# Both halves of an adaLN vector summed by one group of products, two steps after its sums

## The chip, the cores and the metric

The kernel runs on one core of a Trainium2 chip. The core has five engines with a queue of instructions each: TensorE (PE, matmuls), VectorE (DVE), ScalarE (ACT), GpSimd (POOL) and SyncE (SP), which here issues the loads. The metric is the device time of one execution in microseconds.

## What is computed

Two layers of a decoder trunk on `x` of 256 rows by 1024. Each layer runs a first SwiGLU FFN, a token mixer and a second FFN. In front of each of them stands an RMS norm, scaled and shifted by vectors that depend on the condition `c`, and behind each a gate. All of these come from one product per layer:

```python
mod = c_act @ w_ada[l] + b_ada[l]                 # 1024 x 9216
sh1, sc1, g1, sh2, sc2, g2, sh3, sc3, g3 = jnp.split(mod, N_MOD, axis=-1)
x = x + 0.5 * g1 * swiglu(modulate(x, sh1, sc1), ffn1_gate[l], ffn1_up[l], ffn1_down[l])
x = x + g2 * token_mix(modulate(x, sh2, sc2), ...)
x = x + 0.5 * g3 * swiglu(modulate(x, sh3, sc3), ffn2_gate[l], ffn2_up[l], ffn2_down[l])
```

`modulate` is `rms_norm(x) * (1 + scale) + shift`, `swiglu` is `(silu(u @ gate) * (u @ up)) @ down` with 2816 hidden columns. This text calls the nine parts of `mod` chunks 0 to 8. All of it is fp32.

## The kernel before

**Matrix products.** Every fp32 operand is split in two fp32r parts, a rounded high part and the rest. Weights come in loads of up to 1 MB into one of four `raw` buffers (SP, lines 216, 432, 625, 626), and are split there: ACT copies the high part (`whi`, line 177), DVE subtracts it (`wlo`, line 179), each 128x1024 a piece, two pieces a load. PE does three products for each pair of tiles (line 105). A `raw` buffer is free for another load when the last reader on DVE is done, and SP issues loads in one fixed order. A split pair goes into one of seven buffers.

**The vectors of adaLN.** `ada_half` (line 206 on) makes one half, 512 columns, of a chunk: two loads of 1 MB of `w_ada` (line 216), and for each load four scaled additions on DVE into an accumulator `acc` (lines 220 and 222). That leaves 128 partial sums in 128 partitions. Gates (chunks 2, 5 and 8, rows) are then split by ACT (line 229) and DVE (line 230), and two matmuls with a matrix of ones add them up for all partitions; ACT copies the result (line 236). Scales and shifts (columns) go through a `finish`: `column_sums` adds them up with four products of 32 columns into a `tr` bank, eight matmuls in the trace; `pick_columns` takes the wanted elements with a mask on DVE (`mcol`, line 194) and a reduction (`cs`, line 197); `add_bias` writes four columns of `col` (line 203). A `finish` is put in a list and called at the next step of the generator. Ten vectors of columns are made so, in 20 halves.

**Stages.** Chunks 2 to 6 of a layer are made in its first FFN, chunk 7 of layer 0 in its token mixer, and chunk 8 of a layer with chunks 1, 0 and 7 of the next one in its second FFN. (Layer 0's chunks 1 and 0 are made at the start in another way, in `begin`.) Within an FFN the gate and up products run in groups of 256 columns, with one or two steps of the generator (one load of `w_ada` each) per group. Then the down projection runs in two halves of 512 columns (`c = 0, 1`), each of 22 k-tiles in six loads, the last of half size, each load with one step of the generator. Here the six loads of the first half are called D0 to D5, and D6 is the first of the second half. A load feeds 24 matmuls of 128x512. In layer 1's first FFN the chunks come as 2, 3, 4, 5, 6: chunk 4's last half is summed as the gate and up products end, chunks 5 and 6 in the first half of the down projection. At the end of a half the residual is added on DVE (lines 452 and 453).

**What sets the order.** A scheduler orders each engine's queue by its own estimates and by which buffers are free. Each engine does its queue strictly in that order, so an operation that waits holds all that stand behind it on its engine. `acc` has two buffers in the pool `keep`. `sgx` is a tag of the FFN's own pool, with two buffers of the same size, in use by `finish_rows` at the start of an FFN only.

Of the kernel before, what the change touches and what calls it, by code (L numbers as in the profile page):

```python
# [10 lines left out]
F32 = mybir.dt.float32  # L11
# [66 lines left out]
def hybrid_trunk(ctx, tc, t, out):  # L78
# [48 lines left out]
    nc.scalar.activation(cact, c_in, AF.Silu)  # L127
    apart = keep.tile([P, 48], F32, name="apart")
# [57 lines left out]
    def column_sums(ps, vec, a, start, stop):  # L186

        av = a.rearrange("p (j i r) -> p j i r", j=4, i=4)
        for i in range(4):
            mm(ps[32 * i:32 * i + 32, :P].rearrange("p (j r) -> p j r", j=4), vec, av[:, :, i, :], start, stop)  # L190

    def pick_columns(ps):
        m = small.tile([P, 4, 32], F32, name="mcol", tag="mcol", bufs=1)
        nc.vector.tensor_tensor(m, ps[:, :P].rearrange("p (j r) -> p j r", j=4),
                                colmask[:, None, :].to_broadcast([P, 4, 32]), ALU.mult)
        cs = small.tile([P, 4], F32, name="cs", tag="cs", bufs=2)
        nc.vector.tensor_reduce(cs, m, AX.X, ALU.add)
        return cs

    def add_bias(l, ch, n, cs):  # L200
        if (l, ch) not in mods:
            mods[l, ch] = small.tile([P, KD], F32, name="col", tag="col", bufs=8)
        nc.vector.scalar_tensor_tensor(mods[l, ch][:, n * 4:n * 4 + 4], cs, 1.0 if ch in (1, 4, 7) else 0.0,
                                       bcols[:, l, ch * 8 + n * 4:ch * 8 + n * 4 + 4], ALU.add, ALU.add)

    def ada_half(l, ch, n):
        acc = keep.tile([P, 512], F32, name="acc", tag="acc", bufs=2)
        row = ch in (2, 5, 8)
        n0 = ch * D + n * 512
# [15 lines left out]
        if row:  # L225
            if n == 0:
                mods[l, ch] = keep.tile([P, D], F32, name="g", tag="g", bufs=2)
            hi, lo = (scr.tile([P, 512], F32R, name="acc%d" % i, tag="uf", bufs=2) for i in range(2))
# [8 lines left out]
        else:  # L237
            def finish():
                ps = trps()
                column_sums(ps, ones[:, :32].bitcast(F32), acc, True, True)  # L240
                cs = pick_columns(ps)
                add_bias(l, ch, n, cs)
        ada_late.append(finish)
# [4 lines left out]
    def ada_load(chunks):  # L248
        def g():
            for l, ch, n in chunks:  # L250
                for _ in ada_half(l, ch, n):
                    yield
                    while ada_late:
                        ada_late.pop(0)()
# [955 lines left out]
```

## Time and profile before

| what | us |
|---|---|
| median of the three runs | 1186.91 |
| all runs | 2935.22, 1186.91, 1182.08 |
| the profiled execution | 1183.2 |
| its span | 1181.4 |
| granted TensorE clock, mean | 0.999 |

The profile is of one execution. An engine's busy time is given as a share of the span. A wait list names for each engine what it waited for and where. A timeline gives each instruction, or a run of like ones, with its start and duration, and in brackets the idle time ahead of it and what ended it. Consecutive operations on DVE overlap a little, so the distance of two starts says what one of them takes from the engine.

### The profile page before, as it was taken

Reading aid. Unit: us, or ns where it says so; the run is one execution under the profiler, and the core shown is the slowest. Engines: PE = TensorE matmul, PEld = TensorE weight load, DVE = VectorE, ACT = ScalarE, POOL = GpSimd, SP = SyncE. Lnnn points to the kernel's source line nnn. Section 1 sums busy time; section 2 is a strip of 40 time slices with the busy share of each in tenths; the row PEclk is TensorE's granted clock in tenths of the full one; section 3 lists DMA queues with packets and bytes.
Section 4 is the critical chain, followed back from the end, with each engine's and each line's share of the span. In section 5 each row is a group of like instructions: output and inputs, shape, how many; then the busy total and the mean of one; then the engine's idle time right before and its main releaser. Section 6 shows DMA issues by size and latency. Waiting matters only on the chain.

```text
span 1181.4 us, 20214 instructions
## 1 busy us (share of the span) xinstructions
PE 1145.7 (97%) x7886; PEld 1005.9 (85%) x7886; DVE 939.1 (79%) x1889; ACT 642.6 (54%) x1156; POOL 2.5 (0%) x16
## 2 busy tenths in 40 slices
PE   4999999999999999999999999999999999999997
PEld 3799987789967889997879999777997778999985
DVE  4999998778888898798578879975878888865553
ACT  4544544647676564444455534366677756554441
POOL 0000000000000000000000000000000000000000
PEclk9999999999999999999999999999999999999999
DMA  9989999695623578988839979975664354886530
GB/s 330 337 286 330 345 343 332 206 262 174 178 86 102 195 230 290 311 285 314 291 107 295 311 238 360 338 243 167 182 183 108 105 165 157 288 267 211 183 138 36
DMA packets 201970, 274.95 MB, mean 233 GB/s; under 512 B 13613, under 2 KB 119815, under 8 KB 201875
## 3 DMA queue, kind: packets, MB, share of 16 engines
q1 hardware_dynamic: 201119, 273.02, 70.9%
q8 instruction: 62, 1.02, 0.4%
q10 hardware_dynamic: 756, 0.64, 0.2%
q14 instruction: 33, 0.27, 0.1%
HBM read 272.60 MB, written 1.05 MB: 232 GB/s over the span
## 4 chain that ended last, share of the span: by engine, by line
PE 72%; DVE 13%; DMA 8%; ACT 3%; issue 3%; SPq 1%; DVEq 0%; ACTq 0%
PE mm L105 64%; DVE wlo L179 5%; DMA raw<-in_w_ada 4%; DMA raw<-in_ffn_up 3%; PE tr L108 3%; DVE acc L222 3%; PE sc L105 2%; PE po L105 2%; ACT whi L177 1%; PE tr L105 1%; DMA raw<-in_ffn_down 1%; DVE win L724 1%; DVE kd L746 0%; ACT junk L293 0%; DVE hf L494 0%
## 5 line engine op out<-in xcount | busy, mean ns | idle before, releaser
L179 DVE TENSOR_TENSOR wlo<-raw,whi 128x1024 fp32r<-128x1024 f32 (+5 forms) x400 | 423.0, 1073 | 118.0 <-ACT whi L177 115.2
L177 ACT ACTIVATE whi<-raw 128x1024 fp32r<-128x1024 f32 (+5 forms) x400 | 364.3, 936 | 232.4 <-PE mm L105 98.5
L105 PE MATMUL mm<-uhi,whi 128*128 128x256 f32 x1248 | 346.2, 277 | 0.0
L105 PE MATMUL mm<-uhi,wlo 128*128 128x256 f32 x1248 | 345.0, 276 | 0.7 <-DVE wlo L179 0.7
L105 PE MATMUL mm<-ulo,whi 128*128 128x256 f32 x1248 | 344.9, 276 | 0.0
L105 PEld LDWEIGHTS mm<-uhi,whi 128*128 128x128 f32 x1248 | 234.2, 188 | 2.4 <-issue 1.2
L105 PEld LDWEIGHTS mm<-uhi,wlo 128*128 128x128 f32 x1248 | 234.2, 188 | 1.1 <-DVE wlo L179 1.1
L105 PEld LDWEIGHTS mm<-ulo,whi 128*128 128x128 f32 x1248 | 234.4, 188 | 0.5
L222 DVE SCALAR_TENSOR_TENSOR acc<-raw,cact,acc 128x512 f32<-128x512 f32 x224 | 166.9, 747 | 8.7 <-DMA raw<-in_w_ada 5.7
L105 PE MATMUL mm<-whi,hh 128*128 128x512 f32 x352 | 138.2, 393 | 0.0
L105 PE MATMUL mm<-wlo,hh 128*128 128x512 f32 x352 | 137.3, 390 | 0.2 <-DVE wlo L179 0.2
L105 PE MATMUL mm<-whi,hl 128*128 128x512 f32 x352 | 137.1, 389 | 0.0
L105 PE MATMUL mm<-whi,uhi 128*128 128x512 f32 (+3 forms) x336 | 126.3, 378 | 4.4 <-ACT uhi L554 2.6
L105 PE MATMUL mm<-whi,ulo 128*128 128x512 f32 (+3 forms) x336 | 126.3, 377 | 1.5 <-DVE ulo L342 1.5
L105 PE MATMUL mm<-wlo,uhi 128*128 128x512 f32 (+3 forms) x336 | 125.1, 373 | 0.0
L495 ACT ACTIVATE hh<-hf 128x256 fp32r<-128x256 f32 x70 | 29.2, 417 | 103.4 <-DVE hf L494 103.3
L105 PEld LDWEIGHTS mm<-whi,hh 128*128 128x128 f32 x352 | 66.1, 188 | 15.1 <-issue 1.6
L105 PEld LDWEIGHTS mm<-wlo,hh 128*128 128x128 f32 x352 | 66.1, 188 | 14.2 <-DVE wlo L179 0.8
L105 PEld LDWEIGHTS mm<-whi,hl 128*128 128x128 f32 x352 | 66.1, 188 | 13.7
L105 PEld LDWEIGHTS mm<-whi,uhi 128*128 128x128 f32 x336 | 63.3, 189 | 16.1 <-ACT uhi L554 3.0
L105 PEld LDWEIGHTS mm<-whi,ulo 128*128 128x128 f32 x336 | 63.6, 189 | 12.1 <-DVE ulo L342 3.3
L105 PEld LDWEIGHTS mm<-wlo,uhi 128*128 128x128 f32 x336 | 63.6, 189 | 9.5 <-DVE wlo L179 0.2
(248 smaller groups left out, 1327.5 us busy)
## 6 DMA issues: line engine op xcount, KB each, us to landing
raw<-in_w_ada SPq DMA_DIRECT2D x72, 1024.0 KB, 9.0
raw<-in_ffn_gate SPq DMA_DIRECT2D x41, 1024.0 KB, 7.1
raw<-in_ffn_up SPq DMA_DIRECT2D x41, 1024.0 KB, 6.5
raw<-in_ffn_down SPq DMA_DIRECT2D x40, 1024.0 KB, 8.1
raw<-in_w_in SPq DMA_DIRECT2D x18, 1024.0 KB, 6.6
raw<-in_w_in SPq DMA_DIRECT2D x16, 512.0 KB, 6.4
raw<-in_w_out SPq DMA_DIRECT2D x8, 1024.0 KB, 5.1
raw<-in_ffn_down SPq DMA_DIRECT2D x8, 512.0 KB
```

What stands on the lines that cost most here:

```text
L105: last_mm[0] = nc.tensor.matmul(o, a, b, start=start, stop=stop)
L108: nc.tensor.transpose(o, a, ident)
L177: nc.scalar.activation(a, s, AF.Copy)
L179: nc.vector.tensor_tensor(b, s, a.bitcast(F32), ALU.subtract)
L222: nc.vector.scalar_tensor_tensor(acc, rv[:, jj, :], cj, binit if j + jj == 0 else acc, ALU.mult, ALU.add)
L495: nc.scalar.activation(h[0][:, f, :], hf32, AF.Copy)
L724: nc.vector.tensor_tensor(win[i][jj * 64:(jj + 1) * 64, 8 * a:8 * a + 8, g, :], pv[g * 64:(g + 1) * 64, jj, :, a:a + 15], cols[0][jj * 64: ...
```

## The change

`finish` is made once per vector, when both halves are summed. It has eight products in one group, one masked product of 128x256, one reduction to eight columns and one addition of the bias. It is called two steps of the generator behind the end of the sums; the rows' stays at one. Both accumulators are held until then. Every second vector takes its accumulators from `sgx` while an FFN is open, the others from `acc` in `keep`. The tiles with the tag `uf` (`uf`, the rows' split halves, `win`, `pT`, `fnorm`) move from the pool `scr` to the front of `keep`, which shifts the addresses behind it; five more lines like those shown say `keep` for `scr`. Two pads go.

```diff
@@ -125,6 +125,7 @@
     nc.gpsimd.memset(binit, 0.0)
     cact = const.tile([P, KD], F32, name="cact")
     nc.scalar.activation(cact, c_in, AF.Silu)
+    nc.gpsimd.memset(keep.tile([P, 512], F32, name="uf", tag="uf", bufs=2)[:, :1], 0.0)
     apart = keep.tile([P, 48], F32, name="apart")
     nc.gpsimd.memset(apart, 0.0)
     x = keep.tile([P, NH, D], F32, name="x")
@@ -183,29 +184,35 @@
 
     mods = {}
 
-    def column_sums(ps, vec, a, start, stop):
-
-        av = a.rearrange("p (j i r) -> p j i r", j=4, i=4)
-        for i in range(4):
-            mm(ps[32 * i:32 * i + 32, :P].rearrange("p (j r) -> p j r", j=4), vec, av[:, :, i, :], start, stop)
-
-    def pick_columns(ps):
-        m = small.tile([P, 4, 32], F32, name="mcol", tag="mcol", bufs=1)
-        nc.vector.tensor_tensor(m, ps[:, :P].rearrange("p (j r) -> p j r", j=4),
-                                colmask[:, None, :].to_broadcast([P, 4, 32]), ALU.mult)
-        cs = small.tile([P, 4], F32, name="cs", tag="cs", bufs=2)
-        nc.vector.tensor_reduce(cs, m, AX.X, ALU.add)
+    def column_sums(ps, vec, halves):
+
+        for n, a in enumerate(halves):
+            av = a.rearrange("p (j i r) -> p j i r", j=4, i=4)
+            for i in range(4):
+                mm(ps[32 * i:32 * i + 32, n * P:(n + 1) * P].rearrange("p (j r) -> p j r", j=4), vec, av[:, :, i, :],
+                   True, True)
+
+    def pick_columns(ps, n):
+        m = small.tile([P, KD, 32], F32, name="mcol", tag="mcol", bufs=1)
+        nc.vector.tensor_tensor(m[:, :n], ps[:, :n * 32].rearrange("p (j r) -> p j r", j=n),
+                                colmask[:, None, :].to_broadcast([P, n, 32]), ALU.mult)
+        cs = small.tile([P, KD], F32, name="cs", tag="cs", bufs=2)
+        nc.vector.tensor_reduce(cs[:, :n], m[:, :n], AX.X, ALU.add)
         return cs
 
-    def add_bias(l, ch, n, cs):
-        if (l, ch) not in mods:
-            mods[l, ch] = small.tile([P, KD], F32, name="col", tag="col", bufs=8)
-        nc.vector.scalar_tensor_tensor(mods[l, ch][:, n * 4:n * 4 + 4], cs, 1.0 if ch in (1, 4, 7) else 0.0,
-                                       bcols[:, l, ch * 8 + n * 4:ch * 8 + n * 4 + 4], ALU.add, ALU.add)
+
+    acc_rooms = [None]
+    pairs = [0]
+    held = []
 
     def ada_half(l, ch, n):
-        acc = keep.tile([P, 512], F32, name="acc", tag="acc", bufs=2)
         row = ch in (2, 5, 8)
+        if not row and n == 0:
+            pairs[0] += 1
+        if not row and pairs[0] % 2 == 0 and acc_rooms[0] is not None:
+            acc = acc_rooms[0]()
+        else:
+            acc = keep.tile([P, 512], F32, name="acc", tag="acc", bufs=2)
         n0 = ch * D + n * 512
         wv = t["w_ada"][l].rearrange("(p j) n -> p j n", p=P)
         if row:
@@ -225,7 +232,7 @@
         if row:
             if n == 0:
                 mods[l, ch] = keep.tile([P, D], F32, name="g", tag="g", bufs=2)
-            hi, lo = (scr.tile([P, 512], F32R, name="acc%d" % i, tag="uf", bufs=2) for i in range(2))
+            hi, lo = (keep.tile([P, 512], F32R, name="acc%d" % i, tag="uf", bufs=2) for i in range(2))
             nc.scalar.activation(hi, acc, AF.Copy)
             nc.vector.tensor_tensor(lo, acc, hi.bitcast(F32), ALU.subtract)
 
@@ -235,12 +242,20 @@
                 mm(ps, ones, lo, False, True)
                 nc.scalar.activation(mods[l, ch][:, n * 512:(n + 1) * 512], ps, AF.Copy, scale=1.0 if ch == 5 else 0.5)
         else:
+            held.append(acc)
+            if n == 0:
+                return
+            halves = list(held)
+            held.clear()
+
             def finish():
                 ps = trps()
-                column_sums(ps, ones[:, :32].bitcast(F32), acc, True, True)
-                cs = pick_columns(ps)
-                add_bias(l, ch, n, cs)
-        ada_late.append(finish)
+                column_sums(ps, ones[:, :32].bitcast(F32), halves)
+                cs = pick_columns(ps, KD)
+                mods[l, ch] = small.tile([P, KD], F32, name="col", tag="col", bufs=8)
+                nc.vector.scalar_tensor_tensor(mods[l, ch], cs, 1.0 if ch in (1, 4, 7) else 0.0,
+                                               bcols[:, l, ch * 8:ch * 8 + 8], ALU.add, ALU.add)
+        ada_late.append([1 if row else 2, finish])
 
     ada_late = []
     ada_gen = [None]
@@ -250,10 +265,13 @@
             for l, ch, n in chunks:
                 for _ in ada_half(l, ch, n):
                     yield
-                    while ada_late:
-                        ada_late.pop(0)()
+                    for e in list(ada_late):
+                        e[0] -= 1
+                        if e[0] == 0:
+                            ada_late.remove(e)
+                            e[1]()
             while ada_late:
-                ada_late.pop(0)()
+                ada_late.pop(0)[1]()
         ada_gen[0] = g()
 
     def ada_step(n=1):
@@ -468,6 +486,7 @@
             unit_kinds[:] = ["w"] * 4 + ["f"] * EXTRA
             unit_count[0] = 0
             unit_alloc["f"] = lambda: pool_unit(fu)
+            acc_rooms[0] = lambda: fp.tile([P, 512], F32, name="acc", tag="sgx", bufs=2)
             bank_pools[:] = [psum, fps]
             ada_load(ada_plan)
 
@@ -542,11 +561,11 @@
                     accs[q] = acc
 
                 def operands(q):
-                    cs = pick_columns(sums[q])
+                    cs = pick_columns(sums[q], 4)
                     for i, ch in enumerate((1, 0)):
                         nc.vector.scalar_tensor_tensor(mods[l, ch][:, q * 2:q * 2 + 2], cs[:, i * 2:i * 2 + 2], float(ch),
                                                        bcols[:, l, ch * 8 + q * 2:ch * 8 + q * 2 + 2], ALU.add, ALU.add)
-                    uf = scr.tile([P, 2, S], F32, name="uf", tag="uf", bufs=2)
+                    uf = keep.tile([P, 2, S], F32, name="uf", tag="uf", bufs=2)
                     for i in range(2):
                         k = 2 * q + i
                         nc.vector.tensor_scalar(uf[:, i, :], tps[q][:, i * S:(i + 1) * S], mods[l, 1][:, k:k + 1],
@@ -644,6 +663,7 @@
                 xs_gemm(units, ktiles(h[0]), ktiles(h[1]), 512, evac, 6 if c else 0, last if c else None)
             unit_kinds[:] = ["w"]
             bank_pools[:] = [psum]
+            acc_rooms[0] = None
 
 
     def token_mix(l, uhi, ulo, ada_plan, post):
...
@@ -1147,9 +1167,6 @@
-    pad(scr, "before_uf", 320)
-    pad(small, "behind_uf", 192)
```
What this moves on the engines is shown for three places.

**1. A group of column sums, PE, layer 1's first FFN.** `tr` is the bank of the sums, `acc_7968` chunk 4's second half before, `acc_7630` and `acc_7918` its two halves in the change; `whi_8276` is D0's first split before, `whi_8267` D1's in the change. Before:

```order
L105 MATMUL mm_8193<-uhi_6666,wlo_8223 128x256
L105 MATMUL tr_8260<-acc_7968,ones_83 32x128 [waits PE_49]
L105 MATMUL tr_8260<-acc_7968,ones_83 32x128 x3
L105 MATMUL mm_8256<-whi_8276,hh_6763 128x512 [waits Activation_49]
L105 MATMUL mm_8256<-wlo_8277,hh_6763 128x512 [waits DVE_49]
```

In the change:

```order
L105 MATMUL mm_8196<-whi_8221,hl_6720 128x512
L105 MATMUL tr_8239<-acc_7630,ones_83 32x128 x4
L105 MATMUL tr_8239<-acc_7918,ones_83 32x128 x4
L105 MATMUL mm_8195<-whi_8267,hh_6719 128x512 [waits Activation_49]
L105 MATMUL mm_8195<-wlo_8268,hh_6719 128x512 [waits DVE_49]
```

The group has both halves, and stands behind D0's matmuls instead of ahead of them.

**2. The last half of the vectors, DVE, layer 0's second FFN.** `raw_6344` is the third load of the down projection before, `acc_6305` the last half's accumulator:

```order
L179 TENSOR_TENSOR wlo_6329<-raw_6303,whi_6328 128x1024 [waits PE_49,Activation_49]
...
L179 TENSOR_TENSOR wlo_6364<-raw_6344,whi_6363 128x1024 [waits DMAHW7_49,Activation_49]
L179 TENSOR_TENSOR wlo_6380<-raw_6344,whi_6379 128x1024 [waits PE_49,Activation_49]
...
L220 TENSOR_SCALAR acc_6305<-raw_6306,cact_91 128x512 [waits DMAHW6_49]
...
L222 SCALAR_TENSOR_TENSOR acc_6305<-raw_6306,cact_91,acc_6305 128x512 [waits DVE_49] x2
L222 SCALAR_TENSOR_TENSOR acc_6305<-raw_6357,cact_91,acc_6305 128x512 [waits DMAHW0_49,DVE_49]
L179 TENSOR_TENSOR wlo_6408<-raw_6395,whi_6407 128x1024 [waits DMAHW1_49,Activation_49]
L222 SCALAR_TENSOR_TENSOR acc_6305<-raw_6357,cact_91,acc_6305 128x512 [waits DVE_49]
```

In the change the load is `raw_6346`, the accumulator `acc_6267`:

```order
L180 TENSOR_TENSOR wlo_6291<-raw_6250,whi_6290 128x1024 [waits PE_49,Activation_49]
L227 TENSOR_SCALAR acc_6267<-raw_6268,cact_91 128x512 [waits DMAHW6_49]
...
L229 SCALAR_TENSOR_TENSOR acc_6267<-raw_6308,cact_91,acc_6267 128x512 [waits DMAHW0_49,DVE_49]
...
L229 SCALAR_TENSOR_TENSOR acc_6267<-raw_6308,cact_91,acc_6267 128x512 [waits DVE_49]
L180 TENSOR_TENSOR wlo_6364<-raw_6346,whi_6363 128x1024 [waits DMAHW1_49,Activation_49]
L180 TENSOR_TENSOR wlo_6380<-raw_6346,whi_6379 128x1024 [waits Activation_49]
```

The sums, which stood behind the third load's splits, stand ahead of them; PE's products of them, which stood behind the third load's matmuls, stand ahead of these too.

**3. Chunk 5's sums, layer 1's first FFN.** On DVE before, `raw_8258`, `raw_8308` and `raw_8355` are D0, D1 and D2, `acc_8122` and `acc_8315` chunk 5's halves:

```order
L222 SCALAR_TENSOR_TENSOR acc_8122<-raw_8124,cact_91,binit_89 128x512 [waits DMAHW6_49]
...
L222 SCALAR_TENSOR_TENSOR acc_8122<-raw_8124,cact_91,acc_8122 128x512 [waits DVE_49] x2
...
L179 TENSOR_TENSOR wlo_8277<-raw_8258,whi_8276 128x1024 [waits DMAHW7_49,Activation_49]
L179 TENSOR_TENSOR wlo_8293<-raw_8258,whi_8292 128x1024 [waits PE_49,Activation_49]
L222 SCALAR_TENSOR_TENSOR acc_8122<-raw_8270,cact_91,acc_8122 128x512 [waits DMAHW0_49,DVE_49]
...
L179 TENSOR_TENSOR wlo_8324<-raw_8308,whi_8323 128x1024 [waits DMAHW2_49,Activation_49]
L230 TENSOR_TENSOR acc1_8312<-acc_8122,acc0_8311 128x512 [waits Activation_49]
L179 TENSOR_TENSOR wlo_8340<-raw_8308,whi_8339 128x1024 [waits PE_49,Activation_49]
...
L222 SCALAR_TENSOR_TENSOR acc_8315<-raw_8317,cact_91,binit_89 128x512 [waits DMAHW3_49,DMAHW1_49,DVE_49]
...
L179 TENSOR_TENSOR wlo_8368<-raw_8355,whi_8367 128x1024 [waits DMAHW4_49,Activation_49]
L179 TENSOR_TENSOR wlo_8384<-raw_8355,whi_8383 128x1024 [waits PE_49,Activation_49]
```

In the change `raw_8237`, `raw_8299` and `raw_8343` are D1, D2 and D3, `acc_8061` and `acc_8259` chunk 5's halves:

```order
L180 TENSOR_TENSOR wlo_8268<-raw_8237,whi_8267 128x1024 [waits DMAHW1_49,PE_49,Activation_49]
...
L180 TENSOR_TENSOR wlo_8284<-raw_8237,whi_8283 128x1024 [waits PE_49,Activation_49]
...
L180 TENSOR_TENSOR wlo_8312<-raw_8299,whi_8311 128x1024 [waits DMAHW3_49,Activation_49]
L180 TENSOR_TENSOR wlo_8328<-raw_8299,whi_8327 128x1024 [waits PE_49,Activation_49]
...
L229 SCALAR_TENSOR_TENSOR acc_8061<-raw_8063,cact_91,binit_89 128x512 [waits DMAHW6_49,PE_49]
L197 TENSOR_TENSOR mcol_8248<-tr_8239,tab_87 128x256 [waits PE_49]
...
L229 SCALAR_TENSOR_TENSOR acc_8061<-raw_8063,cact_91,acc_8061 128x512 [waits DVE_49]
...
L229 SCALAR_TENSOR_TENSOR acc_8061<-raw_8199,cact_91,acc_8061 128x512 [waits DMAHW0_49,DVE_49]
...
L237 TENSOR_TENSOR acc1_8256<-acc_8061,acc0_8255 128x512 [waits Activation_49]
...
L180 TENSOR_TENSOR wlo_8357<-raw_8343,whi_8356 128x1024 [waits DMAHW6_49]
```

Chunk 5's first sum has a wait for PE now, for the merged group of place 1, and stands behind D2's two splits, where it stood ahead of D0's. SP's queue, before, from the first load of chunk 5 to D3's predecessor:

```order
L216 DMA raw_8124<-in_w_ada 128x4x512 [waits DMAHW2_49,DVE_49]
L432 DMA raw_8258<-in_ffn1_down 128x4x512 [waits DMAHW3_49,DVE_49]
L216 DMA raw_8270<-in_w_ada 128x4x512 [waits DMAHW4_49,DVE_49,Activation_49]
L432 DMA raw_8308<-in_ffn1_down 128x4x512 [waits DMAHW5_49,DVE_49]
L216 DMA raw_8317<-in_w_ada 128x4x512 [waits DMAHW6_49,DVE_49]
L432 DMA raw_8355<-in_ffn1_down 128x4x512 [waits DMAHW7_49,DVE_49]
L216 DMA raw_8361<-in_w_ada 128x4x512 [waits DMAHW0_49,DVE_49]
L432 DMA raw_8399<-in_ffn1_down 128x4x512 [waits DMAHW2_49,DVE_49]
```

In the change (`raw_8197` is D0):

```order
L223 DMA raw_8063<-in_w_ada 128x4x512 [waits DMAHW1_49,DVE_49]
L450 DMA raw_8197<-in_ffn1_down 128x4x512 [waits DMAHW3_49,DVE_49]
L223 DMA raw_8199<-in_w_ada 128x4x512 [waits DMAHW4_49,DVE_49,Activation_49]
L450 DMA raw_8237<-in_ffn1_down 128x4x512 [waits DMAHW5_49,DVE_49]
L223 DMA raw_8261<-in_w_ada 128x4x512 [waits DMAHW7_49,DVE_49]
L450 DMA raw_8299<-in_ffn1_down 128x4x512 [waits DMAHW1_49,DVE_49]
L223 DMA raw_8305<-in_w_ada 128x4x512 [waits DMAHW3_49,DVE_49]
L450 DMA raw_8343<-in_ffn1_down 128x4x512 [waits DMAHW6_49,DVE_49]
```

The sequence is the same, but a load waits for the landing queue (`DMAHW`) of what its buffer held: D2 waits for queue 1, on which D1 landed (DVE's first row above), and D3 for queue 6, on which chunk 5's first load landed. ACT there, in the change:

```order
L178 ACTIVATE whi_8327<-raw_8299 128x1024 [waits PE_49]
L511 ACTIVATE sg_8189<-mm_8132 128x256 [waits PE_49,Activation_49]
L514 ACTIVATE hh_6719<-hf32_8191 128x256 [waits DVE_49]
L219 DMA binit_89<-in_b_ada 1x512 [waits DVE_49]
...
L178 ACTIVATE whi_8356<-raw_8343 128x1024 [waits DMAHW6_49]
L236 ACTIVATE acc0_8255<-acc_8061 128x512 [waits DVE_49]
L178 ACTIVATE whi_8372<-raw_8343 128x1024 [waits PE_49]
```

ACT's half of the row's sum, `acc0_8255`, stands behind D3's first high part, `whi_8356`.

## Rows read from the trace of the kernel before

**Rows 1.** Page, part 1: busy time, share of the span, instructions

```profile
PE 1145.7 (97%) x7886; PEld 1005.9 (85%) x7886; DVE 939.1 (79%) x1889; ACT 642.6 (54%) x1156; POOL 2.5 (0%) x16
```

**Rows 2.** What PE waited for: us in total, times, longest

```profile
PE tr L105 <- DMA raw<-in_w_ada: 10.1, 2, 9.6
PE tr L105 <- DVE acc L541: 2.9, 1, 2.9
...
PE tr L105 <- DVE acc L222: 1.9, 1, 1.9
```

**Rows 3.** PE's timeline at a column group: start, us, engine, line, operation, count

```profile
731.72 0.28 PE L105 MATMUL mm<-ulo,whi 128*128 128x256 f32 x1
731.83 0.28 PE L105 MATMUL mm<-uhi,wlo 128*128 128x256 f32 x1
732.04 0.43 PE L105 MATMUL tr<-acc,ones 128*32 128x128 f32 x8
732.39 0.50 PE L105 MATMUL mm<-whi,hh 128*128 128x512 f32 x1
```

**Rows 4.** Stretch and its us, busy PE, PEld, DVE, ACT, POOL, clock, DMA share, GB/s

```profile
716.00:744.00 28.00, 27.27 (x190) 24.57 (x189) 27.72 (x43) 14.01 (x21) 0.00 (x0) 1.00 1.03 369
```

**Rows 5.** DVE's timeline, layer 0's second FFN, then layer 1's first

```profile
546.19 2.36 DVE L179 TENSOR_TENSOR wlo<-raw,whi 128x1024 fp32r<-128x1024 f32 x2 [1.71 <-ACT whi L177]
...
735.78 1.22 DVE L179 TENSOR_TENSOR wlo<-raw,whi 128x1024 fp32r<-128x1024 f32 x1
736.92 0.42 DVE L494 TENSOR_TENSOR hf<-mm,sg 128x256 f32<-128x256 f32 x1
...
743.28 0.74 DVE L222 SCALAR_TENSOR_TENSOR acc<-raw,cact,acc 128x512 f32<-128x512 f32 x1
743.94 0.42 DVE L496 TENSOR_TENSOR hl<-hf,hh 128x256 fp32r<-128x256 f32 x1
...
763.25 2.36 DVE L179 TENSOR_TENSOR wlo<-raw,whi 128x1024 fp32r<-128x1024 f32 x2 [0.99 <-ACT whi L177]
...
769.72 0.68 DVE L452 TENSOR_TENSOR rtmp<-mm,g 128x512 f32<-128x512 f32 x1
```

**Rows 6.** PE's timeline, first matmuls of D2, then the second of D6

```profile
743.86 0.39 PE L105 MATMUL mm<-whi,hh 128*128 128x512 f32 x1
744.09 0.39 PE L105 MATMUL mm<-wlo,hh 128*128 128x512 f32 x1
...
764.53 0.50 PE L105 MATMUL mm<-wlo,hh 128*128 128x512 f32 x1 [0.24 <-DVE wlo L179]
```

**Rows 7.** By tile, `cs` and `mcol`: duration in ns, min/median/max

```profile
L197 DVE TENSOR_REDUCE cs<-mcol x24: 272/278/286, 16.4 to 778.1; 128x4 f32<-128x128 f32 x24
L203 DVE SCALAR_TENSOR_TENSOR col<-cs,bcols x20: 148/154/164, 116.0 to 779.4; 128x4 f32<-128x4 f32 x20
...
L194 DVE TENSOR_TENSOR mcol<-tr,tab x24: 277/283/286, 16.1 to 776.1; 128x128 f32<-128x128 f32 x24
```

**Rows 8.** ACT's timeline, layer 1's first FFN

```profile
732.64 1.06 ACT L177 ACTIVATE whi<-raw 128x1024 fp32r<-128x1024 f32 x1 [0.51 <-DMA raw<-in_ffn_down]
734.16 0.63 ACT L229 ACTIVATE acc<-acc 128x512 fp32r<-128x512 f32 x1 [0.46 <-DVE acc L222]
```

**Rows 9.** SP's timeline, D2's and D3's loads issued

```profile
730.71 0.37 SPq L432 DMA_DIRECT2D raw<-in_ffn_down  x1
...
737.03 0.37 SPq L432 DMA_DIRECT2D raw<-in_ffn_down  x1
```

**Rows 10.** Page, part 6: loads, count, KB each, median us from issue to landing

```profile
raw<-in_ffn_down SPq DMA_DIRECT2D x40, 1024.0 KB, 8.1
...
raw<-in_w_out SPq DMA_DIRECT2D x8, 1024.0 KB, 5.1
```

**Rows 11.** Columns as in rows 4, the start and the end of the span

```profile
16.00:18.00 2.00, 0.00 (x0) 0.00 (x0) 1.82 (x7) 0.63 (x2) 0.00 (x0) 1.00 1.09 351
...
1179.00:1181.40 2.40, 0.00 (x0) 0.00 (x0) 0.00 (x0) 0.00 (x0) 0.00 (x0) 0.50 0.45 174
```

More of the change, by code (lines that the diff above doesn't have):

```diff
@@ L326, in rest @@
             for b in bs:
-                uf = scr.tile([P, 4, P], F32, name="uf", tag="uf", bufs=2)
+                uf = keep.tile([P, 4, P], F32, name="uf", tag="uf", bufs=2)
                 ps = trps()
@@ L708, in token_mix @@
                 nc.vector.tensor_scalar_mul(cks[:, hf, :256], cks[:, hf, :256], lr[:, 2 + hf:3 + hf])
-            win = [scr.tile([P, 16, 2, 15], F32, name="win%d" % i, tag="uf", bufs=2) for i in range(2)]
+            win = [keep.tile([P, 16, 2, 15], F32, name="win%d" % i, tag="uf", bufs=2) for i in range(2)]
             r = raw_tile()
@@ L966, in transposed @@
                     tr(pt[:, c * P:(c + 1) * P], b)
-                pT = scr.tile([P, 512], F32, name="pT", tag="uf", bufs=2)
+                pT = keep.tile([P, 512], F32, name="pT", tag="uf", bufs=2)
                 if eng is nc.scalar:
@@ L1130, in final_norm @@
             for c in range(2):
-                fnorm[c] = scr.tile([P, 512], F32, name="fnorm%d" % c, tag="uf", bufs=2)
+                fnorm[c] = keep.tile([P, 512], F32, name="fnorm%d" % c, tag="uf", bufs=2)
                 nc.scalar.dma_start(fnorm[c], t["final_norm"].rearrange("(o n) -> o n", o=1)
```

## The prediction, made before the changed kernel ran

> **What bounds the kernel now.** The page comes first: PE is busy 97% of the span, DVE 79% [rows 1]. So the time is PE's own work plus the few waits of PE, and a change is worth what it takes from or adds to these two. Next PE's list of waits: 10.1 us are the first loads of the start, 2.9 us another wait there, and 1.9 us is one wait of a column sum for its accumulator (`acc L222`) [rows 2], and that wait belongs to the operations the change touches. What one group of column products costs PE is read in PE's timeline: the first product starts 0.21 us after the last matmul ahead of it, the next matmul 0.35 us after that, 0.56 us from one to the other, where the matmuls ahead start 0.11 apart [rows 3]. So one group puts in 0.45 us.
>
> Then the stage where the order moves most, layer 1's first FFN from its last gate and up units into the down projection. From 716 to 744 us DVE is busy 27.7 of 28 us and the DMA engines are full (share 1.03, 369 GB/s) [rows 4]. The reader should see that here three things run without slack: loads, DVE's splits and sums, and PE. PE's lead over DVE is short: D1's second split is through at 736.92, where the next operation starts [rows 5], D2's matmuls begin at 743.86 [rows 6], and at D6 the lead is gone, since PE's second matmul there waits 0.24 us for `wlo` [rows 6], whose split starts at 763.25 after a wait for ACT [rows 5].
>
> The profiled execution took 1183.2 us, of which 1181.4 are the span, so 1.8 us lie around it. The median of the runs shown is 1186.9 (1182.1 the lowest): the sum below starts 3.7 us under it, and I keep it there.
>
> **The change, part by part.**
>
> *Products on PE.* Ten vectors have two groups each, 20 x 0.45 = 9.0 us. A merged group keeps one entry and one exit, and adds four fp32 products. Eight matmuls of a group fill 0.43 us against 0.28 for one alone [rows 3], so seven steps take 0.15 us, eight more some 0.17; with one more gap of 0.11 between the halves I take 0.26, so a merged group is 0.71 and a vector saves 0.19: **-1.9 us**. Bounds: nothing, if every product costs as now (0.90), and 10 x (0.90 - 0.62) = 2.8. Why a group costs more than its matmuls is a rule in the Trainium skill, TensorEngine Tiling (Array Packing), section Key Properties: changing the tiling mode drains the engine. By that rule the two borders are paid once per group and the saving is the 1.9; if the products themselves were dear, it would be 0. The rows favour the rule: entry and exit take the larger part of the 0.45.
>
> *Picking on DVE.* Per half 283 + 278 + 154 ns [rows 7], per vector 1.43 us. Merged, both wide operations double to 256 elements, where another two-input operation of 128x256 takes 0.42 [rows 5]; 0.42 + 0.42 + 0.16 = 1.0, so 0.43 us a vector, 4.3 in all. PE covers it, since DVE is not the bound over most of the span; 0 in the sum (at most the 0.43 of the one vector in the full stretch).
>
> *The wait of 1.9 us.* It stands in layer 0's second FFN: DVE idles 1.71 us for ACT before two splits at 546.19 [rows 5] and then does the last half's sums among later splits, and PE's products wait. In the new order the second half's sums stand ahead of the third load's splits, where DVE idled, and the products after them. **-1.9 us**; bounds 0 (the splits become late instead) and 1.9.
>
> *Edits at nothing.* The two pads and their memsets against one memset of a column: POOL has 2.5 us in all, at the start [rows 1]. Moving `uf`, `win`, `pT`, `fnorm` shifts addresses, and adds no instruction and no queue entry. SP issues the same loads in the same sequence.
>
> *The accumulators held longer.* This is the price. A vector now holds two accumulators until two steps after its sums. In layer 1's first FFN chunk 3 draws from `sgx`, chunk 4 from `keep`, and chunk 5, a row vector, needs both `keep` buffers that chunk 4 holds. Its first sum therefore waits for the merged products, and stands behind D2's two splits; its raw buffers stay full. The order shows what follows: D2's load waits for D1's landing queue, so it takes D1's own buffer, where before it took D0's; D3's load waits for the queue of chunk 5's first load, so it takes the buffer that the late sums read. I follow it in trace times:
>
> 1. D1's splits end at 736.9 as now, since D1's landing sets them (`whi` waits for it until 732.64 [rows 8]). D2 is issued there and not at 730.71 [rows 9]: 6.3 us later.
> 2. The queue runs empty by then, so landing takes not the 8.1 us of the page's median for `ffn_down` but about the 5.1 of `w_out`, the shortest of the loads of 1 MB [rows 10]: 742.0. `whi` 1.06 [rows 8], `wlo` 1.14 (735.78 to 736.92): 744.2, the second 745.4. PE, with its group moved behind D0, starts D0 0.45 before the 732.39 of [rows 3] and reaches D2 at 731.9 + 5.45 + 0.71 + 5.45 = 743.5 (24 matmuls a load, 0.227 apart as the two in [rows 6]) and waits 0.7.
> 3. The last `hf` and `hl`, 0.7, then four sums with the pick between them, 4 x 0.66 (a sum followed by another operation, 743.28 to 743.94 [rows 5]) + 0.8 = 3.4: 749.5. Only then is D3 issued, now 737.03 [rows 9]: 12.5 late.
> 4. D3 lands at 754.6; `whi` to 755.6; ACT's half of the row sum stands behind it, to 756.3 (0.63, now done at 734.16 [rows 8]); DVE's half 0.6 (a like operation of 128x512 takes 0.68 with its end overlapped [rows 5]), one sum 0.66, `wlo` 1.14: 758.7. The row's products stand inside D2's last matmuls, so PE stops there already. D3 starts at 758.7 instead of 743.86 + 5.45 = 749.3: **+9.4 us**.
> 5. D4's split stands behind four more sums: +0.8. At D6 DVE now does the residual's four operations (0.68 alone, from 769.72 now [rows 5]) ahead of D6's first split, where before two loads' splits went first; PE runs dry there for about 1.7 us against 0.24 now, +1.5; and D6's second split comes after three sums: +0.8.
>
> Sum of the stall: **+12.5 us**. Its two unloaded landings are the weak numbers. With 4.0 us each and D2 issued a microsecond sooner it is near 8, with the 8.1 of the page's `ffn_down` [rows 10] near 18. After D6 the DMA engines have room again and the lost time is not given back, because PE itself was idle.
>
> Total: 1183.2 - 1.9 - 1.9 + 12.5 = **1191.9, forecast 1192 us**.
>
> **The rivals.**
>
> *No new stall.* If DVE finds its data early enough, only the savings are left: 1183.2 - 3.8 = 1179. For it: DVE has 0.43 us a vector less to do, and the products that chunk 5 waits for are through PE at 738.2, long before DVE comes there. Against: the raw buffers, not PE, pace the loads, and that is order, not speed. 0.14.
>
> *The group saves nothing.* Entry and exit are paid per half; the change does not do its part on PE and the stall stays: 1194. 0.10.
>
> *The clock falls, and it ends slower.* At 1179 to 1181.4, when PE has done its last matmul, the granted clock is 0.50, the lower of its two levels [rows 11]. A stop of 9 us at D3 is longer than any that PE has now after the first loads, where 2.9 is the longest [rows 2]. If PE came back at 1.2 GHz, D3's 5.45 us would become 10.9, and if the rest of the down projection (30 us) ran so, +30: 1222. It decides from about 19 us of work at the lower level, since 1192 + 19 is 2% over. Against: the 2 us at 16 to 18 without a matmul show 1.00 [rows 11], and from D3 on PE is loaded without a break again. The Trainium skill, TensorE: Matmul & The Clock Gate, Part 1, has the rule that the throttled state is the default and activity releases it; by it some microseconds after the stop would be slow, which makes 1194 to 1197, and a whole slow stage is unlikely. The fall of the clock after the last matmul agrees with it; no row here shows a return. 0.04 for the slow stage.
>
> **How the numbers follow.** The forecast as told, 1186 to 1201 with its bounds, gets 0.72; the three rivals 0.14, 0.10 and 0.04. Range 1180 to 1201: it takes in the unmeasured landings on one side and most of the case without a stall on the other. A measurement of this kernel tells about 2%, 24 us, from no change: below 1163 no case lies, 0.01; above 1211 the clock case and a stall half as long again, 0.05; within, 0.94.
>
> **What would show it.** In the new profile: column groups at 0.7 us and ten of them; the `acc` wait near 556 gone; in SP's timeline D2 issued near 737 and D3 near 749; DVE idle before D2's splits; and PE's list of waits led, after the start, by the row products or `wlo` with some 9 us. The prediction is wrong if D3 is issued before 744, if PE stops at less than 3 us there, or if a stop shows in another stage, which I have not found in the order.

## The result: 1.1% slower, and the profile after

| | before | the change |
|---|---|---|
| median us (runs) | 1183.81 (6) | 1194.91 (6) |
| profiled execution, its span | 1183.2, 1181.4 | 1192.4, 1190.6 |
| mean granted clock of that execution | 0.999 | 0.993 |

The ratio of the runs is 1.0106, with an interval from 1.0081 to 1.0130. One run of before, 2935 us, is a disturbed one and is left out of the ratio; the median of the other five is 1182.59, and against it the change costs 12.3 us, clear of the noise and within 2%.

The page of the change, part 1's line and the clock in slices, against [rows 1]:

```profile
PE 1149.5 (97%) x7886; PEld 1010.1 (85%) x7886; DVE 938.3 (79%) x1859; ACT 642.3 (54%) x1156; POOL 2.4 (0%) x15
...
PEclk9999999999999999999999999899999999999999
```

PE works 3.8 us longer in the profile's count, with the same number of instructions, and the clock now has a slice under 0.9. PE's list of waits, against [rows 2] (us in total, times, longest):

```profile
PE tr L105 <- ACT acc L236: 5.9, 1, 5.9
...
PE mm L105 <- ACT whi L178: 2.8, 1, 2.8
```

The wait of 1.9 us for `acc L222` has gone. A wait of 5.9 us has come, for ACT's half of a row sum (line 236 is line 229 of before), and one of 2.8 us for a high part. Both lie in layer 1's first FFN. SP there, D1's, D2's and D3's loads, the last two against [rows 9]; D1's stood at 725.00 before. (The last load of each of the two SP lists under "The change" is D3 itself, not its predecessor.)

```profile
718.56 0.37 SPq L450 DMA_DIRECT2D raw<-in_ffn_down  x1
...
731.29 0.37 SPq L450 DMA_DIRECT2D raw<-in_ffn_down  x1
...
744.63 0.37 SPq L450 DMA_DIRECT2D raw<-in_ffn_down  x1
```

D0's matmuls begin at 728.88 in this run, at 732.39 before. Taken from there, D2 is issued 2.4 us behind them (before, 1.7 ahead), and D3 15.8 behind (before, 4.6). D1 is issued 10.3 us ahead of them, where before it was 7.4. DVE and ACT, against [rows 5] and [rows 8] (start, us, then the idle time ahead in brackets):

```profile
737.57 2.36 DVE L180 TENSOR_TENSOR wlo<-raw,whi 128x1024 fp32r<-128x1024 f32 x2 [5.06 <-ACT whi L178]
...
741.09 0.75 DVE L229 SCALAR_TENSOR_TENSOR acc<-raw,cact,binit 128x512 f32<-128x512 f32 x1
```

```profile
736.47 2.01 ACT L178 ACTIVATE whi<-raw 128x1024 fp32r<-128x1024 f32 x2 [4.42 <-DMA raw<-in_ffn_down]
...
749.57 1.06 ACT L178 ACTIVATE whi<-raw 128x1024 fp32r<-128x1024 f32 x1 [8.85 <-DMA raw<-in_ffn_down]
750.53 0.61 ACT L236 ACTIVATE acc<-acc 128x512 fp32r<-128x512 f32 x1
...
769.92 0.63 ACT L311 ACTIVATE junk<-x 128x512 f32<-128x512 f32 x1 [6.85 <-DVE x L471]
...
770.55 1.04 ACT L178 ACTIVATE whi<-raw 128x1024 fp32r<-128x1024 f32 x1
```

DVE waits 5.06 us for D2's high part, ACT 4.42 us for D2 and 8.85 us for D3; for D1 it waited 0.51 before [rows 8]. Chunk 5's first sum is at 741.09. Before, it was ahead of D0's matmuls:

```profile
724.89 0.75 DVE L222 SCALAR_TENSOR_TENSOR acc<-raw,cact,binit 128x512 f32<-128x512 f32 x1
```

At 749.57 D3's high part comes, and right behind it, as the order had it, ACT's half of the row sum. PE (9 of its rows, from D0's first matmul, against [rows 6]):

```profile
728.88 0.39 PE L105 MATMUL mm<-whi,hh 128*128 128x512 f32 x1
...
744.95 0.39 PE L105 MATMUL mm<-wlo,hh 128*128 128x512 f32 x1
751.20 0.79 PE L105 MATMUL tr<-acc,ones 128*128 128x512 f32 x1 [5.87 <-ACT acc L236]
751.79 0.63 PE L105 MATMUL mm<-whi,hl 128*128 128x512 f32 x1
752.22 0.63 PE L105 MATMUL mm<-whi,hh 128*128 128x512 f32 x1
...
754.76 0.40 PE L105 MATMUL mm<-wlo,hh 128*128 128x512 f32 x1
755.00 0.39 PE L105 MATMUL mm<-whi,hl 128*128 128x512 f32 x1
...
771.64 1.11 PE L105 MATMUL mm<-whi,hh 128*128 128x512 f32 x2 [2.75 <-ACT whi L178]
773.06 0.79 PE L105 MATMUL mm<-wlo,hh 128*128 128x512 f32 x1 [0.31 <-DVE wlo L180]
```

Behind the matmul that starts at 744.95 PE stands until 751.20. What it does then starts 0.43 apart, and only from 754.76 on 0.23 again. At D6 it stands again for 2.75 us and then works at 0.43. The stretches say why (columns as in [rows 4]; the column ahead of the DMA share is the clock):

```profile
716.00:744.00 28.00, 28.00 (x190) 25.00 (x189) 15.66 (x25) 9.73 (x15) 0.00 (x0) 1.00 0.57 190
...
749.00:751.00 2.00, 0.00 (x0) 0.00 (x0) 1.97 (x4) 1.43 (x2) 0.00 (x0) 0.50 0.26 23
751.00:755.00 4.00, 3.80 (x10) 3.00 (x10) 4.00 (x6) 1.93 (x4) 0.00 (x0) 0.53 0.97 364
771.00:775.00 4.00, 3.04 (x7) 1.94 (x8) 3.88 (x8) 3.86 (x8) 0.00 (x0) 0.60 1.05 390
```

From 716 to 744 DVE is busy 15.7 of 28 us and the DMA share is 0.57, against 27.7 and 1.03 [rows 4]: the stretch that had no slack has lost half of its work, because the loads don't come. And the clock falls to 0.50, the lower of its two levels, in the stop, is at 0.53 on average right after it, and at 0.60 after the second stop.

A merged group on PE (against [rows 3]), and picking on DVE (against [rows 7]; min/median/max in ns):

```profile
734.13 0.39 PE L105 MATMUL mm<-whi,hl 128*128 128x512 f32 x1
734.45 0.64 PE L105 MATMUL tr<-acc,ones 128*32 128x128 f32 x16
735.03 0.50 PE L105 MATMUL mm<-whi,hh 128*128 128x512 f32 x1
```

```profile
L200 DVE TENSOR_REDUCE cs<-mcol x14: 286/411/420, 17.1 to 780.2; 128x8 f32<-128x256 f32 x10, 128x4 f32<-128x128 f32 x4
L256 DVE SCALAR_TENSOR_TENSOR col<-cs,bcols x10: 157/162/168, 139.5 to 781.7; 128x8 f32<-128x8 f32 x10
```

From the last matmul ahead to the first behind are 0.90 us, of which 0.23 are a plain step: 0.67 us for a vector, where two halves took 0.90. The mask and the reduction take 0.42 and 0.41 on 256 elements and the bias 0.16, together 0.99 for a vector and not 1.43.

### The profile page after: what moved, and what is told of

Its sections match the earlier page's. It is cut to its first block, busy times and chain, and to the rows that moved or that the text cites. A ratio compares the mean times of both kernels' runs of the same rounds, so it can differ in the third digit from the quotient of the medians.

```text
span 1190.6 us, 20182 instructions
## 1 busy us (share of the span) xinstructions
PE 1149.5 (97%) x7886; PEld 1010.1 (85%) x7886; DVE 938.3 (79%) x1859; ACT 642.3 (54%) x1156; POOL 2.4 (0%) x15
## 4 chain that ended last, share of the span: by engine, by line
PE 73%; DVE 11%; DMA 8%; ACT 4%; issue 3%; SPq 1%; DVEq 0%; ACTq 0%
PE mm L105 65%; DVE wlo L180 4%; DMA raw<-in_w_ada 4%; PE tr L108 3%; DMA raw<-in_ffn_up 3%; PE sc L105 2%; PE po L105 2%; DVE acc L229 2%; ACT whi L178 2%; PE tr L105 1%; DMA raw<-in_ffn_down 1%; DVE win L744 1%; DVE rtmp L470 0%; DMA c_in<-in_c 0%; ACT junk L311 0%
## 5 line engine op out<-in xcount | busy, mean ns | idle before, releaser
L105 PEld LDWEIGHTS mm<-whi,ulo 128*128 128x128 f32 x336 | 63.9, 190 | 11.8 <-DVE ulo L360 3.1
```

The source lines that it names most:

```text
L105: last_mm[0] = nc.tensor.matmul(o, a, b, start=start, stop=stop)
```

## The experiments

Each was compared with runs of the kernel before on its own chip. "Stage" is the time from D0's first matmul to the last one of the down projection in layer 1's first FFN, read from PE's timeline of the one profile: 63.46 us before (732.39 [rows 3] to 795.85), 76.19 in the change (728.88 to 805.07). The last matmul of each, before first:

```profile
795.85 0.39 PE L105 MATMUL mm<-whi,hl 128*128 128x512 f32 x1
```

```profile
805.07 0.40 PE L105 MATMUL mm<-whi,hl 128*128 128x512 f32 x1
```

| kernel | median us | ratio | interval | stage us |
|---|---|---|---|---|
| the change | 1194.9 | 1.0106 | 1.0081 to 1.0130 | 76.2 |
| e1_reset | 1182.4 | 0.9992 | 0.9977 to 1.0007 | 63.7 |
| e2_delay1 | 1192.7 | 1.0076 | 1.0053 to 1.0098 | 74.0 |
| e3_room | 1182.2 | 0.9992 | 0.9973 to 1.0011 | 62.9 |
| e4_delay3 | 1194.6 | 1.0102 | 1.0074 to 1.0130 | 76.6 |
| e5_filler | 1196.3 | 1.0108 | 1.0080 to 1.0136 | 76.9 |
| e7_tm_halves | 1181.4 | 0.9984 | 0.9967 to 1.0001 | 63.3 |
| e8_halves1 | 1181.6 | 0.9989 | 0.9974 to 1.0004 | 62.6 |
| e9_filler40 | 1196.8 | 1.0112 | 1.0082 to 1.0141 | 75.2 |
| e10_six_first | 1184.6 | 1.0011 | 0.9994 to 1.0028 | 65.9 |

### e1_reset: chunk 4 from the other room

```diff
             acc_rooms[0] = lambda: fp.tile([P, 512], F32, name="acc", tag="sgx", bufs=2)
+            pairs[0] = 0
```

> The changed kernel with one line more: the count of vectors starts again at zero with each FFN, so that in layer 1's first FFN chunk 4 draws from sgx and chunk 5's row finds both keep accumulators free. Theory 1 (chunk 5 waits for chunk 4's held accumulators, its loads stay in their buffers, D2 and D3 come late, PE stops): no stop of PE over 1 us between 716 and 790 us, D3 issued near 737 us, granted clock 1.00 there, and only the savings left: ratio to the kernel before 0.995 to 0.999, about 1180 us. Theory 2 (the change costs elsewhere: the moved tiles, the merged products or the two steps as such): no better than 1.006, 1190 us or more.

0.9992: the whole loss is gone with one line that only swaps two rooms in layer 1. SP and two stretches of this kernel:

```profile
729.78 0.37 SPq L450 DMA_DIRECT2D raw<-in_ffn_down  x1
...
736.13 0.37 SPq L450 DMA_DIRECT2D raw<-in_ffn_down  x1
```

```profile
744.00:765.00 21.00, 21.00 (x94) 17.25 (x93) 19.03 (x26) 7.73 (x10) 0.00 (x0) 1.00 0.97 346
255.00:260.00 5.00, 5.00 (x27) 5.00 (x28) 2.45 (x4) 3.02 (x5) 0.00 (x0) 0.66 1.31 248
```

D2 and D3 are issued 1.2 us ahead of and 5.1 behind D0's matmuls (731.02), as before; the clock is 1.00 there, and PE's wait list has no entry between 716 and 765. Theory 1 holds for the loss. The savings, expected with a ratio of 0.995 to 0.999, did not show: 0.9992, with an interval that takes in 1. In the profiled execution a part of them was lost as the last row has it: the clock was 0.66 at 255 to 260 us, behind a wait of 1.9 us in layer 0's token mixer. The kernel before has that wait too, with 1.7 us and a clock of 1.00 in its profile.

### e10_six_first: the rooms as they are, chunk 6 ahead of chunk 5

```diff
-            ffn(l, 1, u[0], u[1], HALVES(l, 2, 3, 4, 5, 6), post,
+            ffn(l, 1, u[0], u[1], HALVES(l, *((2, 3, 4, 5, 6) if l == 0 else (2, 3, 4, 6, 5))), post,
```

> The changed kernel with its rooms as they are, but in layer 1's first FFN chunk 6 comes ahead of chunk 5. Chunk 6 draws from sgx, which is free, and when chunk 5 comes, chunk 4's products are done. Theory 1 (the hold of chunk 4's accumulators over chunk 5's first sums makes the stop): no stop over 1 us between 716 and 790 us, the same loads issued within 1 us of e1_reset's distance to D0's matmuls, ratio 0.998 to 1.001. Rival (the rooms in sgx or the merged finish itself make the order that stops PE): the stop stays, 1.006 or more.

The second way round the hold, with the rooms of the change. The stop at D2 and D3 is gone, and the ratio of 1.0011 lies a hair above the expected 0.998 to 1.001, with an interval that covers it. D2 is issued 1.5 us ahead of D0's matmuls, within 1 us of e1_reset as expected, D3 3.5 behind them, which is 1.6 earlier than there and not within 1 us. "No stop over 1 us" was wrong too: the row's sums are now the last of the stage, and PE waits 1.8 us for them at D6:

```profile
770.61 0.39 PE L105 MATMUL mm<-whi,hl 128*128 128x512 f32 x1
772.77 0.50 PE L105 MATMUL tr<-acc,ones 128*128 128x512 f32 x1 [1.77 <-ACT acc L236]
```

The two kernels agree: what stops PE is that a row needs accumulators which the vector ahead of it still holds.

### e2_delay1 and e4_delay3: one step, three steps

```diff
-        ada_late.append([1 if row else 2, finish])
+        ada_late.append([1, finish])                     # e2_delay1
+        ada_late.append([1 if row else 3, finish])       # e4_delay3
```

> The changed kernel with the columns' finish one step behind the sums instead of two; the pair of accumulators and their rooms as in the change. Theory 1: chunk 5 still finds both keep accumulators held, its first sum stands between D2's two splits, where it stood behind both, and PE still stops at the row's products for 3 to 6 us: 1188 to 1194 us. Theory 3 (the second step alone makes the stop): the stop is gone, 1179 to 1183 us.

> The changed kernel with the columns' finish three steps behind the sums. Theory 1 with the order of DVE as what sets the end (chunk 5's first sum stands behind D2's splits in either case, and D2's landing, not the products, releases it): the stop at the row's products stays at 5 to 7 us, 1192 to 1198 us. If the products release it, the stop grows by up to a load's matmuls, 5.45 us: 1198 to 1203 us.

PE's waits from 716 to 800 us, e2_delay1 first, then e4_delay3:

```profile
PE tr L105 <- ACT acc L236: 5.9, 1, 5.9
```

```profile
PE mm L105 <- ACT whi L178: 6.3, 2, 4.2
PE mm L105 <- DVE wlo L180: 1.7, 2, 1.0
```

One step still gives a stop of 5.9 us, as expected. Three steps cost no more than two, also as expected (1194.6), but the place was wrong: PE stops not at the row's products but at D3's first matmul, 4.2 us for its high part. With the other waits of up to 2.1 it comes to 8.0 us, against 9.0 in the change, and the stage is 0.4 us longer. In the three kernels chunk 5's first sum starts 7.6 (one step), 12.2 (two) and 11.8 us (three) behind D0's first matmul, and before it started 7.5 us ahead of it. So the second step is not needed for the loss, and in the change it isn't PE's products that release the sum: those start at 734.45, the sum at 741.09, behind D2's splits. What the sum waits for there is its place in DVE's queue, behind work that D2's landing releases. That the scheduler gave it this place because of its wait for the products is argued from the order, and not tested by itself.

### e3_room: the rooms alone

```diff
 the kernel before, with
-            hi, lo = (scr.tile([P, 512], F32R, name="acc%d" % i, tag="uf", bufs=2) for i in range(2))
+            hi, lo = (keep.tile([P, 512], F32R, name="acc%d" % i, tag="uf", bufs=2) for i in range(2))
...
-    pad(scr, "before_uf", 320)
-    pad(small, "behind_uf", 192)
```

> The kernel before with only the rooms moved: the tiles with the tag uf in keep, the memset of a column, the two pads gone; sums and finish as before. Theory 1: the same time within the interval, ratio 0.998 to 1.002, and the wait of 1.9 us near 556 us still there. Theory 2 in its form with addresses: a good part of the change's 1.0106, 1.004 or more.

0.9992: the moved tiles do nothing that can be measured. PE's wait near 556 us is there, with 0.7 us in this execution and not 1.9:

```profile
PE tr L105 <- DVE acc L223: 0.7, 1, 0.7
```

### e5_filler and e9_filler40: work for PE in the stop

```diff
                 ps = trps()
+                if (l, ch, n) == (1, 5, 0):
+                    for _ in range(24):                  # 40 in e9_filler40
+                        mm(ps.rearrange("p (k n) -> p k n", k=2), ones, full[0][:, 0:2, :], True, True)
                 mm(ps, ones, hi, True, False)
```

`full[0]` is the high part of the hidden rows, which is ready.

> The changed kernel with 24 matmuls of 128x512 more on PE, which write the bank of chunk 5's first row sum just ahead of its products and are overwritten by them: 5.45 us of PE work placed where PE stops 5.9 us. If the clock's fall is a consequence of that stop and has a price of its own: the granted clock stays 1.00 from 744 to 760 us, the matmuls after the row's products start 0.227 apart instead of 0.43, and the kernel is 1 to 2 us faster than the changed kernel although PE does 5.45 us more: 1191 to 1194 us, span of the profile 1188 to 1190. If the fall has nothing to do with the stop: the filler fits into the wait, the clock falls all the same, the same time as the change within 1 us.

The filler did not do what it was made for. The scheduler put it ahead of D2's matmuls, so PE came to the row's products earlier and still waited. PE in e5_filler:

```profile
744.93 5.60 PE L105 MATMUL tr<-hh,ones 128*128 128x512 f32 x24
754.34 0.50 PE L105 MATMUL tr<-acc,ones 128*128 128x512 f32 x1 [3.80 <-ACT acc L237]
...
756.02 0.63 PE L105 MATMUL mm<-whi,hh 128*128 128x512 f32 x1
756.45 0.63 PE L105 MATMUL mm<-wlo,hh 128*128 128x512 f32 x1
...
761.57 0.40 PE L105 MATMUL mm<-wlo,hh 128*128 128x512 f32 x1
761.80 0.40 PE L105 MATMUL mm<-whi,hl 128*128 128x512 f32 x1
```

After waits of 3.8 and 0.59 us the clock falls, for 13 matmuls, and the ratio is that of the change within its interval. So the first form of the expectation failed, and this kernel alone settles nothing. The second one was longer:

> As e5_filler, with 40 matmuls (9.1 us) in place of 24. In e5_filler the filler ran ahead of D2's matmuls, PE still waited 3.8 us behind it and the clock fell again, for 12 matmuls at 0.43. If the wait makes the clock fall, the longer filler takes it away: under 1 us of wait is left before the row's products, the granted clock is 1.00 from 744 to 765 us, the matmuls behind the products start 0.227 apart, and the stage is 2 to 2.6 us shorter than in e5_filler, although PE does 3.6 us more. If the fall does not hang on the wait, the matmuls behind are at 0.43 as before and the stage stays as long or grows.

```profile
742.25 9.23 PE L105 MATMUL tr<-hh,ones 128*128 128x512 f32 x40
752.77 0.50 PE L105 MATMUL tr<-acc,ones 128*128 128x512 f32 x1 [1.30 <-ACT acc L237]
754.16 0.50 PE L105 MATMUL tr<-acc,ones 128*128 128x512 f32 x1 [0.89 <-DVE acc L238]
754.50 0.39 PE L105 MATMUL mm<-whi,hh 128*128 128x512 f32 x1
754.72 0.39 PE L105 MATMUL mm<-wlo,hh 128*128 128x512 f32 x1
```

With 9.1 us of filler the waits are 1.3 and 0.89 us, and the matmuls behind start 0.23 apart. The stage is 1.75 us shorter than in e5_filler with 3.6 us more work in it (2 to 2.6 were expected, and less waiting), and 1.0 shorter than in the change with 9.1 more. So in these profiles the fall hangs on how long PE stands. The medians of the two fillers don't differ (1196.3 and 1196.8): the price of the fall is read from single executions, at 0.2 us for a matmul of 512 columns.

### e7_tm_halves and e8_halves1: the token mixer's order, and a better version

```diff
 e1_reset, with
         else:
+            if acc_rooms[0] is None:        # the token mixer: a half by itself, as before
...
+                    column_sums(ps, ones[:, :32].bitcast(F32), [acc])
+                    cs = pick_columns(ps, 4)
...
+                ada_late.append([1, finish])
+                return
```

and e8_halves1 has `ada_late.append([1, finish])` for the merged vectors too.

> The changed kernel with the count of vectors starting again at each FFN (as in e1_reset), and chunk 7 in layer 0's token mixer done per half and one step behind its sums as in the kernel before. DVE's queue in that token mixer is then, row for row, that of the kernel before. If the 1.2 us that the changed kernels lose there come from the order that the scheduler makes of it: they are back, and the ratio to the kernel before is 0.996 to 0.999 (1179 to 1182 us). If not: as e1_reset, 0.999.

> As e7_tm_halves, with the finish of the merged vectors one step behind the sums instead of two. If the second step is what takes away PE's wait near 556 us for the last accumulator: that wait is back with 0.9 to 2.1 us, and the time is 1 to 2 us above e7_tm_halves. If merging alone does it: the same as e7_tm_halves.

The first transposes of `cqs` and the next stage's first of `sgx`, in the kernel before and then in the change:

```profile
272.61 0.60 PE L108 MATMUL tr<-ident,cqs 128*128 128x128 f32 x4
...
432.56 0.60 PE L108 MATMUL tr<-ident,sgx 128*128 128x128 f32 x4
```

```profile
271.85 0.60 PE L108 MATMUL tr<-ident,cqs 128*128 128x128 f32 x4
...
432.96 0.63 PE L108 MATMUL tr<-ident,sgx 128*128 128x128 f32 x4
```

From the one to the other are 159.95 us before and 161.11 in the change. e1_reset has 161.17 and e2_delay1, with one step, 161.23; e3_room has 159.89, e7_tm_halves 159.91 (271.98 to 431.89) and e8_halves1 159.96. So the 1.2 us come with merging in the token mixer, with one step as with two, and without it they are gone. Chunk 7's own work lies ahead of that stretch, its last operation on DVE at 263.5 in the change. That the loss comes by another order of the attention's small operations is argued and not shown. The ratio of e7_tm_halves is the lowest of all and within the expected band; against the kernel before the interval ends at 1.0001, so it is faster by 0.2% at the most likely and not clearly so, and the intervals of e7_tm_halves and e1_reset overlap. e8_halves1 is the same within the interval, and has no wait near 556 us either: the wait goes with merging, with one step as with two.

## Why the prediction was right, and where it was not

**The direction and the size.** 1192 was forecast, 1194.9 is the median, and the profiled execution took 1192.4. The sum closes in the profiles: PE comes to D0 3.5 us earlier than before (728.88 for 732.39; the savings were put at 3.8), the stage takes 76.19 - 63.46 = 12.7 more (+12.5 was forecast), and behind it nothing changes: 385.5 us from the last matmul of the stage to the end of the span in both. That the total comes out within half a microsecond is luck in two ways. The profiled execution of the change is the fastest of its six, and by the medians the change costs 12.3 us where the sum had 8.7. And the terms inside the 12.5 were wrong in both directions.

**The accumulators.** The mechanism is right, and shown by e1_reset and e10_six_first. The trace has it as told: D2 is issued at 731.29, when DVE's second split of D1 ends (730.04 and 1.22 us), D3 at 744.63, when the fourth sum of chunk 5 ends (743.86 and 0.75 us). The two unloaded landings, called the weak numbers and put at 5.1 us, took 5.2 (731.29 to 736.47) and 4.9 (744.63 to 749.57).

Step 1 failed in its time. It left the end of D1's splits at 736.9, 5.0 us behind the D0 of step 2 (731.9). They end at 731.26, 2.4 behind D0. Chunk 5's sums no longer stand ahead of D0's splits on DVE, and D0 and D1 are issued 9.5 and 6.4 us earlier than before (709.79 for 719.33, 718.56 for 725.00), which the step did not look at. So the times in the prediction (D2 at 737, D3 at 749) are some 5 us too high: 3 because D0 came earlier than the 731.9, the rest because of D1. D3's load, by the steps 13.0 us late against D0, is 11.1 late; its 744.6 is only just on the right side of the 744 that was named as the mark of a failure.

**The make-up of the 12.7.** Here terms were mis-sized, and cancelled. Step 4 had PE 9.4 us late at D3, all of it waiting; PE waits 5.9. Step 5 had 0.8 at D4, where PE doesn't wait, and 1.5 and 0.8 at D6; there PE waits 2.75 + 0.31 against 0.24, because ACT, too, does the residual's square (769.92) ahead of D6's high part (770.55), which the step had not looked at. The rest is the clock: from 751.20 to 754.76 eight steps take 3.56 us and not 1.82, and from 771.64 to 775.30 seven take 3.66, less the 0.31 of waiting, and not 1.59. Together about 3.5 us. With 0.4 for the group that now lies in this stage it makes 5.9 + 2.8 + 3.5 + 0.4 = 12.6. Two readings in the prediction were loose as well: with landings of 4.0 us and D2 a microsecond sooner its own numbers give 12.5 - 2.2 - 1.0 = 9.3 and not 8; and the end of D1's splits was set against D2's matmuls, while D2's splits end at 742.8, 1.1 us ahead of them.

**The clock.** It fell, and the sum had nothing for it; the rival was priced only as a whole slow stage. After a stop it lasts here for 7 to 13 matmuls. The rule of the Trainium skill, TensorE: Matmul & The Clock Gate, Part 1, that the throttled state is the default and activity releases it, was weighed in a sentence that gave 1194 to 1197; the trace agrees, with 0.50 in the stop and 0.53 after it, and the median lies in that band. The row held against it, 1.00 with PE idle from 16 to 18 us, was weak evidence, as in e5_filler's execution the same start has a clock of 0.74 and 0.57 at 15 to 25 us.

**The products.** Forecast 0.71 us a group, measured 0.67; 0.23 saved a vector, so -2.3 for ten against -1.9. The rule of the Trainium skill, TensorEngine Tiling (Array Packing), Key Properties, that a change of tiling mode drains the engine, fits: twice the products add 0.22 us to the 0.45 of a group.

**The wait of 1.9.** It went. But it was one execution's figure: e3_room shows 0.7 for the same order, so it is worth 0.7 to 1.9.

**What was said to cost nothing.** The rooms do (e3_room). The picks on DVE save 0.44 us a vector, as forecast. PE's two waits for `wlo` ahead of D0 (0.7 us before) are gone too, but e3_room, with the groups as before, doesn't have them either, so merging need not be the reason. Against that stands a loss in another stage, of the kind that the prediction had "not found in the order": layer 0's token mixer, +1.2 us, of which 0.6 are waits of PE, none of those added over 0.3, so it is no stop. The sum had nothing for it. It takes a good part of what merging saves; e1_reset, which has it, stands at 0.9992, and e7_tm_halves, which hasn't, at 0.9984, though their intervals overlap.

## What to carry to other kernels

Before results are held longer, list who asks for the same buffers next and what that one frees: here a sum that waited for an accumulator kept a load buffer, and the loads behind it fed PE. Where buffers alternate between two rooms by a count, follow the count through all stages; the same code made no such stop in layer 0 and cost 12.7 us in layer 1. A change of one helper moves a scheduler's order far from its place, so compare the stages that should not change, too.

## What the runs showed of the hardware

- A stop of PE costs more than its length: after waits of 5.9, 2.75 and 3.8 us the granted clock is at 0.5 to 0.6, and the next 7 to 13 matmuls of 512 columns start 0.43 us apart instead of 0.23. After waits of 1.3 and 0.89 us in a row (e9_filler40), and after 1.77 (e10_six_first, clock 1.00 at 772 to 776 us), they started 0.23 apart.
- The same wait may or may not have that price. Behind a wait of 1.7 us near 253 us the clock was 1.00 in the profile of before, behind one of 1.9 us at the same place it was 1.00 in e9_filler40 and 0.66 for 5 us in e1_reset. Executions of the change have mean clocks from 0.988 to 0.993 and times from 1192 to 1202 us, those of before 0.992 to 0.999 and 1179 to 1189.
- 9.1 us of matmuls that nothing needs made the stage no longer in e9_filler40's profile: 75.2 us against 76.2 in the change.
- A load of 1 MB takes 4.9 to 5.2 us from issue to its first reader in the change, when the loads behind it are held up, and 8.1 in the median of `ffn_down` before [rows 10].
